# A mixed prompt and decode step: top-k masks made with ScalarE's sign pass and queued later, values in two products per key tile

## Chip, core and metric

The kernel runs on one core of a Trainium2 chip. The metric is the device time of one execution in microseconds (us). Times named "span" are the length of the profiled execution from its first to its last instruction.

## What is computed

One layer for 1024 prompt frames and 8 x 16 sampled frames that continue running streams (128 rows together, so nine tiles of 128 rows; tile 8 is the sampled one). Half of the mixing width is a gated recurrence, the other half sparse attention; both go through one output matrix, and a SwiGLU network follows. The part that the change touches is the attention. For each query row an index score is computed against all keys, and only the best 256 keys (132 for the sampled rows) take part; ties are broken by position:

```
idx_score = einsum('bths,bth->bts', relu(sc), wi)
idx_score = where(adm, idx_score, -inf)          # a chunk sees itself and what is before it
vals, sel = top_k(idx_score, topk)
s = einsum('bthgd,btkhd->bthgk', qg, ks) * HEAD_DIM ** -0.5
p = softmax(where(valid, s, -inf))
o = einsum('bthgk,btkhd->bthgd', p, vs)          # 8 query heads, 2 key/value heads of 64
...
x = x + concat([y_a, y_b]) @ w_out
x = x + (silu(gu[:, :D_FF]) * gu[:, D_FF:]) @ w_ffn_out
```

Results are wanted at float32 precision. The kernel's matmuls work on numbers split into a high and a low part, three products (low x high, high x low, high x high) for one.

## The kernel before

Work is written as generators, one per tile and stage. A planner (`run`) keeps its own clocks for the engines, steps several of them in turn and so fixes the order in which instructions are issued; a scheduler of the compiler then places them per engine. Each engine works through its own queue in that order, and an instruction that waits holds up all behind it. The stages are: norms and keys/values per tile; index scores; the recurrence and the query projections; the first half of the output projection (`out_tile_a`, the recurrence's half of w_out); attention (`attn` for eight prompt tiles times two key/value groups, `sample_attn` for eight streams); the second half of the output projection (`out_tile`); the feed-forward network. Threshold search and masks (`topk`) run beside them as side work, in two groups: tiles 2 to 5, counted on ScalarE ("act"), and tiles 6 to 8, counted on VectorE. Tiles 0 and 1 take part whole.

`topk_mask` turns the scores `s` of a tile into 0 for selected keys and -2^100 for others. With the threshold v it makes eq = (s == v) on VectorE (into the scratch `jk1` or `junk`), a running count of eq by a scan (into PSUM for tiles 2 to 5, into `key` for 6 to 8), the pass s > v with its count (VectorE, float32, in place), the number c of ties still to take (`tk_cnt`), and the selection of the first c ties; GpSimd then adds eq to s and scales:

```
nc.vector.tensor_scalar(eq, s, v, None, op0=ALU.is_equal)
nc.vector.tensor_tensor_scan(rk, e, e, a, op0=ALU.add, op1=ALU.max)
nc.vector.tensor_scalar(s, s, v, None, op0=ALU.is_gt, op1=ALU.add, accum_out=c)
nc.vector.scalar_tensor_tensor(e, rk, c, e, op0=ALU.is_le, op1=ALU.mult)
self.pool_tt(s, s, eq, ALU.add)
```

At the same time `out_tile_a` multiplies `yF` with `wa` (float32, 128x512) into two PSUM banks per tile and VectorE adds them to `acc`; `k_rope` rotates and scales the keys `kn` (VectorE and GpSimd), TensorE transposes them, ScalarE and VectorE split them into `k1` and `k2`; `q_norm` scales the queries `qn` on GpSimd. All PSUM tiles come in turn from one ring of eight banks, those of the scans too. `sample_prep` copies the mask of tile 8 (`junk<-s`) and a pattern (`key<-ident`) once all masks are there.

In `attn`, for each query tile i and group kv of four heads: scores in PSUM (`k`, `qeo`), mask and maximum on VectorE, exponentials on ScalarE, scaling on GpSimd (`m`), then for each key tile kt four transpositions, a split into high and low parts (`rest`, `smr`: ScalarE copies, VectorE subtracts), and `mm3` with the values `vhl` into one bank `po`, three matmuls of 512 columns. The stationary operand holds both groups' values, 128 columns, of which one group's 64 are used: ScalarE copies half of `po` into `yF`. Tiles 0 to 5 come first, tiles 6 and 7 among the streams.

Of the kernel before, what the change touches and what calls it, by code (L numbers as in the profile page):

```python
# [14 lines left out]
AF = mybir.ActivationFunctionType  # L15
# [6 lines left out]
NT = 9  # L22
NP = 8
# [58 lines left out]
class Kernel:  # L82
# [183 lines left out]
    def build(self, upto=99):  # L266
# [44 lines left out]
        self.jk = [self.junk.bitcast(BF16), tka_p.tile([128, widest[1]], BF16, name="jk1")]  # L311
        self.scored, self.masked, self.tk_done = set(), {0, 1}, set()
        self.qst, self.qst_t = {}, {}
        self.n_lru, self.spare = 0, None
        self.m_turn, self.m_next, self.n_sa, self.in_att, self.k_done = 0, 0, 0, False, False
        self.n_idx, self.n_sidx, self.sidx, self.sq_done = 0, 0, None, False
        topks = [self.topk(g, p) for g, p in zip(groups, self.TK_PACE)]
# [235 lines left out]
    def norm_kv(self, i, tp, g, wk):  # L553
# [25 lines left out]
        for a in range(2):  # L579
            nc.scalar.activation(sq[:, a * 64:a * 64 + 64], kv[:, a * 64:a * 64 + 64], AF.Square, scale=0.125,  # L580
                                 accum_out=self.kss[:, i, a:a + 1])
        self.hi(self.vhl[:, i, 0, :], kv[:, 128:256], "pool")
        self.lo(self.vhl[:, i, 1, :], kv[:, 128:256], self.vhl[:, i, 0, :])
        vo = O["v_p"][0, i * 128:(i + 1) * 128] if i < NP else O["v_s"].rearrange("b t k d -> (b t) k d")
        nc.sync.dma_start(vo.rearrange("t k d -> t (k d)"), kv[:, 128:256])
        nc.gpsimd.tensor_scalar(self.wi[:, i, :], kv[:, 320:328], 8.0 ** -0.5 * 64.0 ** -0.5, 0.0,
# [203 lines left out]
    def topk(self, g, pace):  # L790
# [41 lines left out]
                yield pace  # L832
        self.topk_threshold(g)
        yield pace
        for j in range(g["n"]):
            self.topk_mask(g, j)
            self.masked.add(g["tiles"][j])
            yield pace
        self.tk_done.add(g["id"])
# [45 lines left out]
    def topk_threshold(self, g):  # L885
        nc = self.nc
        v, c, t, T = g["v"], g["c"], g["t"], g["cand"].bitcast(F32)
        if not g["act"]:
            nc.vector.scalar_tensor_tensor(v, t, 2.0 ** -22, c, op0=ALU.mult, op1=ALU.add)
            nc.vector.scalar_tensor_tensor(v, v, 0.5, g["e"].bitcast(F32), op0=ALU.mult, op1=ALU.mult)  # L890
            return
        nc.vector.tensor_scalar(v, T, -1.0, None, op0=ALU.mult)
        for j, i in enumerate(g["tiles"]):
            w = self.s[i].shape[1]
            nc.vector.tensor_scalar(self.jk[1][:, :w], self.s[i], v[:, j:j + 1], None, op0=ALU.is_gt, op1=ALU.add,
                                    accum_out=c[:, j:j + 1])

        nc.vector.tensor_scalar(c, c, 256.0, 2.0 ** -24 * (1 + 2.0 ** -20), op0=ALU.is_ge, op1=ALU.mult)
        nc.vector.scalar_tensor_tensor(t, v, -1.0, v, op0=ALU.mult, op1=ALU.max)
        nc.vector.tensor_tensor(t, t, c, op=ALU.mult)  # L900
        nc.vector.tensor_tensor(v, v, t, op=ALU.add)

        nc.vector.scalar_tensor_tensor(t, v, -1.0, v, op0=ALU.mult, op1=ALU.max)
        nc.vector.tensor_scalar(t, t, 1.1754944e-38, None, op0=ALU.is_gt)
        nc.vector.tensor_tensor(v, v, t, op=ALU.mult)

    def topk_mask(self, g, j):

        nc = self.nc
        i = g["tiles"][j]  # L910
        s = self.s[i]
        w = s.shape[1]
        k = 132 if i == NP else 256
        v, c = g["v"][:, j:j + 1], g["c"][:, j:j + 1]
        eq = self.jk[1 if g["act"] else 0][:, :w]
        nc.vector.tensor_scalar(eq, s, v, None, op0=ALU.is_equal)
        rks, a = [], 0.0
        for o in range(0, w, 512 if g["act"] else w):
            e = eq[:, o:min(w, o + 512)] if g["act"] else eq
            rk = self.ps()[:, :e.shape[1]] if g["act"] else g["keys"][j]  # L920
            nc.vector.tensor_tensor_scan(rk, e, e, a, op0=ALU.add, op1=ALU.max)
            a = rk[:, -1:]
            rks.append((rk, e))
        nc.vector.tensor_scalar(s, s, v, None, op0=ALU.is_gt, op1=ALU.add, accum_out=c)
        nc.vector.tensor_scalar(c, c, -1.0, float(k), op0=ALU.mult, op1=ALU.add)
        for rk, e in rks:
            nc.vector.scalar_tensor_tensor(e, rk, c, e, op0=ALU.is_le, op1=ALU.mult)
        self.pool_tt(s, s, eq, ALU.add)
        nc.gpsimd.tensor_scalar(s, s, BIG, -BIG, op0=ALU.mult, op1=ALU.add)


# [395 lines left out]
    def out_tile_a(self, i):  # L1327

        nc = self.nc
        nc.sync.dma_start(self.acc[i], self.x_src(i))  # L1330
        w = []
        pos = [self.ps(), self.ps()]
        for c in range(4):
            w += yield from self.wait_w(("wa", c))
            for q in range(2):
                self.mm4(pos[q], self.yF[:, c, i * 128:(i + 1) * 128], w[c][:, q * 512:(q + 1) * 512], c == 0, c == 3)
            yield 0.0
        if i == NT - 1:
            self.wused -= 4
        for q in range(2):  # L1340
            a = self.acc[i][:, q * 512:(q + 1) * 512]
            nc.vector.tensor_tensor(a, pos[q], a, op=ALU.add)
            yield 0.4 if q else 0.0

    def out_tile(self, i, tp):
# [26 lines left out]
    def attn(self, i, kv, tp):  # L1372
# [57 lines left out]

        def product(kt):
            x, pT = pTs.pop(kt)
            self.mm3(po, self.vhl[:, kt, 0, :], self.vhl[:, kt, 1, :], pT[:, 0], pT[:, 1], kt == 0, kt == i)
            self.pT_free.append(x)

        for kt in range(i + 1):
# [13 lines left out]
                yield 0.0  # L1450
        yield from self.until(ready[i])
        product(i)
        a = slice(64 * kv, 64 * kv + 64)
        nc.scalar.activation(self.yF[a, :, i * 128:(i + 1) * 128], po[a].rearrange("p (j t) -> p j t", j=4), AF.Copy)

    def sample_prep(self):
        nc = self.nc
# [279 lines left out]
```

## Time and profile before

| | |
|---|---|
| median of 3 runs | 1557.31 us (1556.19 to 1558.42) |
| profiled execution | 1558.3 us, span 1556.1 us |
| mean granted TensorE clock | 0.977 of 2.4 GHz |
| busy: TensorE, VectorE, ScalarE, GpSimd | 95%, 56%, 39%, 18% |

The profiled execution is one run with its trace. Busy shares are means over stages with different limits: from about 672 us on, TensorE works on without a break and the other engines have little to do; before that VectorE and ScalarE are often the fuller ones. A busy TensorE is not one at its peak: matmuls are pipelined, and one that stands alone is counted with its whole latency. A matmul in plain float32 shows as two records. A row of the trace that ends in brackets tells how long its engine was idle before it and whose work released it.

### The profile page before, as it was taken

Reading aid. Unit: us, or ns where it says so; the run is one execution under the profiler, and the core shown is the slowest. Engines: PE = TensorE matmul, PEld = TensorE weight load, DVE = VectorE, ACT = ScalarE, POOL = GpSimd, SP = SyncE. Lnnn points to the kernel's source line nnn. Section 1 sums busy time; section 2 is a strip of 40 time slices with the busy share of each in tenths; the row PEclk is TensorE's granted clock in tenths of the full one; section 3 lists DMA queues with packets and bytes.
Section 4 is the critical chain, followed back from the end, with each engine's and each line's share of the span. In section 5 each row is a group of like instructions: output and inputs, shape, how many; then the busy total and the mean of one; then the engine's idle time right before and its main releaser. Section 6 shows DMA issues by size and latency. Waiting matters only on the chain.

```text
span 1556.1 us, 20869 instructions
## 1 busy us (share of the span) xinstructions
PE 1477.2 (95%) x7786; PEld 1313.2 (84%) x7786; DVE 876.0 (56%) x1909; ACT 613.5 (39%) x1467; POOL 274.0 (18%) x425
## 2 busy tenths in 40 slices
PE   6889899889869999999999999999999999999998
PEld 6777688778525788889999998989898989898987
DVE  7556899889986988677233333342424242414143
ACT  6447988987203977655202020212021212111100
POOL 4214233334882444300000000000000000000000
PEclk9999899999979999999999999999999999999999
DMA  7201111001400002122102020202020111111003
GB/s 240 57 16 35 42 37 30 14 21 62 163 19 16 1 15 69 28 68 73 64 0 82 0 82 1 82 2 81 16 67 27 55 40 43 49 33 55 28 1 122
DMA packets 95093, 75.24 MB, mean 48 GB/s; under 512 B 13380, under 2 KB 85828, under 8 KB 94992
## 3 DMA queue, kind: packets, MB, share of 16 engines
q1 hardware_dynamic: 94992, 73.91, 15.7%
q8 instruction: 61, 1.00, 0.3%
q14 instruction: 40, 0.33, 0.1%
HBM read 67.62 MB, written 6.27 MB: 47 GB/s over the span
## 4 chain that ended last, share of the span: by engine, by line
PE 74%; DVE 12%; ACT 7%; issue 4%; POOL 1%; DMA 1%; SPq 0%; ACTq 0%; DVEq 0%; POOLq 0%
PE ps L207 67%; DVE junk L66 4%; PE ps L212 4%; PE ps L217 3%; ACT jk L66 3%; DVE tk_cand L66 2%; ACT m L66 1%; ACT L66 1%; DVE s L66 1%; DVE tr L66 1%; ACT tr L66 1%; DVE qn L66 1%; ACT relu L66 1%; POOL qn L66 0%; DMA x<-in_x_prompt_dram 0%
## 5 line engine op out<-in xcount | busy, mean ns | idle before, releaser
L207 PE MATMUL ps<-hf,w 128*128 128x384 f32 x2556 | 460.6, 338 | 0.0
L207 PEld LDWEIGHTS ps<-hf,w 128*128 128x128 f32 x2556 | 451.5, 187 | 0.8
L207 PE MATMUL ps<-w,a 128*128 128x512 f32 x999 | 239.1, 390 | 0.0
L66 DVE TENSOR_TENSOR acc<-ps,acc 128x512 f32<-128x512 f32 x234 | 160.9, 690 | 120.4 <-PE ps L207 119.1
L207 PEld LDWEIGHTS ps<-w,a 128*128 128x128 f32 x999 | 187.4, 188 | 40.1
L66 DVE TENSOR_TENSOR sg<-ps,sg 128x384 f32<-128x384 f32 x66 | 36.8, 557 | 280.2 <-PE ps L207 279.6
L66 ACT ACTIVATE w<-raw 128x512 fp32r<-128x512 f32 x124 | 75.2, 628 | 300.2 <-PE ps L207 220.6
L66 DVE TENSOR_TENSOR w<-raw,w 128x512 fp32r<-128x512 f32 x116 | 76.8, 687 | 85.1 <-ACT w L66 84.9
L66 ACT ACTIVATE a<-sg 128x384 fp32r<-128x384 f32 x66 | 34.5, 523 | 221.2 <-DVE sg L66 221.2
L207 PE MATMUL ps<-hf,rest 128*128 128x384 f32 x612 | 114.5, 334 | 0.0
L66 ACT ACTIVATE jk<-s,tk_cand 128x384 bf16<-128x384 f32 (+3 forms) x128 | 99.4, 776 | 31.9 <-DVE tk_cand L66 29.3
L207 PE MATMUL ps<-h,w 128*128 128x384 f32 x576 | 107.3, 344 | 0.0
L207 PEld LDWEIGHTS ps<-hf,rest 128*128 128x128 f32 x612 | 106.9, 188 | 0.2
L207 PEld LDWEIGHTS ps<-h,w 128*128 128x128 f32 x576 | 101.0, 188 | 3.9 <-ACT relu L66 0.2
L207 PE MATMUL ps<-w,h 128*128 128x256 f32 (+1 forms) x600 | 95.5, 314 | 0.0
L207 PEld LDWEIGHTS ps<-w,h 128*128 128x128 f32 x600 | 82.8, 188 | 6.6
L66 ACT ACTIVATE sg<-ps 128x384 f32<-128x384 f32 x66 | 32.0, 485 | 121.9 <-PE ps L207 121.9
L212 PE MATMUL ps<-wa,yF 128*128 128x512 f32 x144 | 67.7, 626 | 3.1 <-DVE acc L66 2.2
L212 PEld LDWEIGHTS ps<-wa,yF 128*128 128x128 f32 x144 | 28.2, 202 | 38.5 <-issue 32.8
L66 POOL TENSOR_SCALAR m<-m,mx 128x128 f32<-128x128 f32 (+7 forms) x64 | 47.4, 748 | 64.7 <-DVE mx L66 57.3
L207 PE MATMUL ps<-smr,vhl 128*128 128x512 f32 x162 | 54.0, 419 | 1.3 <-ACT smr L66 1.1
L66 DVE TENSOR_TENSOR a<-sg,a 128x384 fp32r<-128x384 f32 x66 | 36.8, 557 | 32.6 <-ACT a L66 32.6
(261 smaller groups left out, 2163.7 us busy)
## 6 DMA issues: line engine op xcount, KB each, us to landing
raw<-in_w_ffn_in_dram SPq DMA_DIRECT2D x44, 512.0 KB, 4.7
raw<-in_w_ffn_out_dram SPq DMA_DIRECT2D x22, 512.0 KB, 3.6
raw<-in_w_in_dram SPq DMA_DIRECT2D x16, 512.0 KB, 5.0
out_dram<-acc SPq DMA_DIRECT2D x9, 512.0 KB, 2.6
x<-in_x_prompt_dram SPq DMA_DIRECT2D x8, 512.0 KB
acc<-in_x_prompt_dram SPq DMA_DIRECT2D x8, 512.0 KB
tab<-in_rope_dram SPq DMA_DIRECT2D x43, 64.0 KB, 1.7
wa<-in_w_out_dram SPq DMA_DIRECT2D x4, 512.0 KB
```

Source lines behind the costliest of these rows:

```text
L66: return f(*args, **kw)
L207: self.nc.tensor.matmul(out, lhsT, rhs, start=start, stop=stop)
L212: self.nc.tensor.matmul(out, lhsT, rhs, start=start, stop=stop)
L217: self.nc.tensor.transpose(out, in_, self.ident[0:n, 0:n])
```

## The change

Three things. First, a mask's equality and greater-than passes on VectorE are replaced: ScalarE computes sign(s - v) with its sum n (`topk_threshold` now leaves -v in `t` for it), VectorE compares the signs with 0, and the ties to take follow from n and the number of ties a. For tiles 2 to 5 the signs stand in s itself; for tiles 6 to 8 they stand as bf16 in the second half of the scratch `junk`, beside eq in its first half. Second, masks of tiles 6 to 8 are issued only after the last sum of `out_tile_a` (`wa_last`), in the order of every engine. Third, the values of the prompt tiles are stored as [high of a group | low of that group], 64 columns each, so that one matmul with the high part of p and one with its low part give all four products; the two halves of `po` then have to be added: ScalarE copies one half, VectorE adds the other.

```diff
@@ norm_kv
-        self.hi(self.vhl[:, i, 0, :], kv[:, 128:256], "pool")
-        self.lo(self.vhl[:, i, 1, :], kv[:, 128:256], self.vhl[:, i, 0, :])
+        v, vs = self.vhl[:, i], kv[:, 128:256]
+        if i < NP:
+            v = v.rearrange("p a (x d) -> p x a d", x=2)
+            vs = vs.rearrange("p (a d) -> p a d", a=2)
+        self.hi(v[:, 0], vs, "pool")
+        self.lo(v[:, 1], vs, v[:, 0])
@@ topk
         self.topk_threshold(g)
         yield pace
+        if not g["act"]:
+            while self.wa_last is None:
+                yield 0.5
         for j in range(g["n"]):
-            self.topk_mask(g, j)
+            with ExitStack() as st:
+                if not g["act"]:
+                    st.enter_context(self.tc.issue_after(self.wa_last))
+                self.topk_mask(g, j)
@@ topk_threshold (both groups)
+            nc.vector.tensor_scalar(t, v, -1.0, None, op0=ALU.mult)
@@ topk_mask
-        v, c = g["v"][:, j:j + 1], g["c"][:, j:j + 1]
-        eq = self.jk[1 if g["act"] else 0][:, :w]
-        nc.vector.tensor_scalar(eq, s, v, None, op0=ALU.is_equal)
+        c, eq, n = g["c"][:, j:j + 1], self.jk[1 if g["act"] else 0][:, :w], g["cnt"][:, j:j + 1]
+        sg = s if g["act"] else self.jk[0][:, 1024:1024 + w]
+        nc.scalar.activation(sg, s, AF.Sign, bias=g["t"][:, j:j + 1], accum_out=n)
+        nc.vector.tensor_scalar(eq, sg, 0.0, None, op0=ALU.is_equal)
         ...
-        nc.vector.tensor_scalar(s, s, v, None, op0=ALU.is_gt, op1=ALU.add, accum_out=c)
-        nc.vector.tensor_scalar(c, c, -1.0, float(k), op0=ALU.mult, op1=ALU.add)
+        nc.vector.tensor_tensor(c, n, a, op=ALU.subtract)
+        nc.vector.tensor_scalar(c, c, -0.5, k - 0.5 * w, op0=ALU.mult, op1=ALU.add)
         for rk, e in rks:
             nc.vector.scalar_tensor_tensor(e, rk, c, e, op0=ALU.is_le, op1=ALU.mult)
-        self.pool_tt(s, s, eq, ALU.add)
+        self.pool_tt(s, sg, eq, ALU.add)
@@ out_tile_a
-            nc.vector.tensor_tensor(a, pos[q], a, op=ALU.add)
+            x = nc.vector.tensor_tensor(a, pos[q], a, op=ALU.add)
+            if q and i == NT - 1:
+                self.wa_last = x.ins
@@ attn, product
-            self.mm3(po, self.vhl[:, kt, 0, :], self.vhl[:, kt, 1, :], pT[:, 0], pT[:, 1], kt == 0, kt == i)
+            for q in range(2):
+                self.mm(po, self.vhl[:, kt, kv], pT[:, q], kt == 0 and q == 0, kt == i and q == 1)
@@ attn, end
-        a = slice(64 * kv, 64 * kv + 64)
-        nc.scalar.activation(self.yF[a, :, i * 128:(i + 1) * 128], po[a].rearrange("p (j t) -> p j t", j=4), AF.Copy)
+        a, b = (slice(64 * x, 64 * x + 64) for x in (kv, 1 - kv))
+        y = self.yF[a, :, i * 128:(i + 1) * 128]
+        nc.scalar.activation(y, po[b].rearrange("p (j t) -> p j t", j=4), AF.Copy)
+        nc.vector.tensor_tensor(y, po[a].rearrange("p (j t) -> p j t", j=4), y, op=ALU.add)
```

Up to the end of the recurrence the order of instructions stays as it was. In VectorE's queue the first sums of the output projection stood like this before (s4 and s7: scores of tiles 4 and 7; a scan shows as SCALAR_TENSOR_TENSOR with one input):

```order
L66 SCALAR_TENSOR_TENSOR junk_911<-key_1983,tk1_cnt_905,junk_911 128x1024
L66 TENSOR_TENSOR tail_91<-tail_91 128x72
L66 TENSOR_TENSOR qn_1945<-qn_1945,tab_4134 128x256
L66 SCALAR_TENSOR_TENSOR ps_4370<-jk1_912 128x512
L66 TENSOR_SCALAR s4_890,tk0_cnt_896<-s4_890,tk0_cnt_896 128x640
L66 TENSOR_TENSOR kn_88<-kn_88,tab_4437 128x128
L66 TENSOR_TENSOR acc_4027<-ps_4360,acc_4027 128x512
L66 CAST key_1983<-ident_84 128x1024
L66 TENSOR_SCALAR tail_91<-tail_91 128x72
L66 TENSOR_TENSOR qn_1945<-qn_1945,rp_4233 128x256
L66 TENSOR_TENSOR acc_4027<-ps_4361,acc_4027 128x512
```

The same place in VectorE's queue of the changed kernel:

```order
L66 TENSOR_SCALAR jk1_912<-s5_891 128x768
L66 TENSOR_TENSOR qss_1944<-tail_91 128x72
L66 SCALAR_TENSOR_TENSOR ps_4397<-jk1_912 128x512
L66 SCALAR_TENSOR_TENSOR ps_4399<-jk1_912,ps_4397 128x256
L66 TENSOR_TENSOR acc_4007<-ps_4343,acc_4007 128x512
L66 TENSOR_TENSOR tk0_cnt_896<-tk0_cnt_896,ps_4399 128x1
L66 TENSOR_TENSOR acc_4007<-ps_4344,acc_4007 128x512
L66 TENSOR_TENSOR qn_1945<-qn_1945,tab_4169 128x256
L66 TENSOR_SCALAR tk0_cnt_896<-tk0_cnt_896 128x1
L66 TENSOR_TENSOR qn_1945<-qn_1945,rp_4257 128x256
L66 SCALAR_TENSOR_TENSOR jk1_912<-ps_4397,tk0_cnt_896,jk1_912 128x512
```

Tile 7's passes and the pattern's copy have left this place, and tile 5's have come ahead of the first sum. At the start of attention VectorE's queue went from the last sum straight to the queries' split and the first scores before:

```order
L66 TENSOR_TENSOR acc_4337<-ps_4654,acc_4337 128x512
L66 TENSOR_TENSOR ksT_4343<-ps_4685,ksT_4343 128x128
L66 TENSOR_TENSOR rest_4026<-ps_4698,rest_4026 64x4x8x16
L66 TENSOR_TENSOR qeo_4715<-ps_4710,qeo_4715 64x512 x2
L66 TENSOR_TENSOR qeo_4725<-ps_4720,qeo_4725 64x512 x2
L66 ISA m_4730,mx_4731<-ps_4732,kn_88 128x128
```

VectorE's queue at the same place now (junk and key are the scratch and the count of tile 6):

```order
L66 TENSOR_TENSOR acc_4320<-ps_4639,acc_4320 128x512
L66 TENSOR_SCALAR junk_911<-junk_911 128x896
L66 TENSOR_TENSOR ksT_4326<-ps_4670,ksT_4326 128x128
L66 SCALAR_TENSOR_TENSOR key_1983<-junk_911 128x896
L66 TENSOR_TENSOR qeo_4687<-ps_4682,qeo_4687 64x512 x2
L66 TENSOR_TENSOR tk1_cnt_905<-tk1_cnt_905,key_1983 128x1
L66 TENSOR_TENSOR qeo_4697<-ps_4692,qeo_4697 64x512 x2
L66 ISA m_4710,mx_4711<-ps_4712,kn_88 128x128
```

Tile 6's equality, scan and count now stand among the first splits and scores; those of tiles 7 and 8 follow between the scores of tiles 0 to 3. GpSimd's queue there, before, goes from filling the fixed mask of tiles 0 and 1 to the softmax scalings:

```order
L66 MEMSET kn_88 128x128
L66 MEMSET kn_88 128x256
L66 MEMSET kn_88 64x64
L66 TENSOR_SCALAR m_4730<-m_4730,mx_4731 128x128
L66 TENSOR_SCALAR m_4730<-m_4730,mx_4739 128x128
L66 TENSOR_SCALAR m_4747<-m_4747,mx_4748 128x128
```

And GpSimd's queue now:

```order
L66 MEMSET kn_88 128x256
L66 MEMSET kn_88 64x64
L66 TENSOR_TENSOR s6_892<-junk_911 128x896
L66 TENSOR_SCALAR m_4710<-m_4710,mx_4711 128x128
L66 TENSOR_SCALAR m_4710<-m_4710,mx_4727 128x128
L66 TENSOR_SCALAR m_4735<-m_4735,mx_4736 128x128
```

The mask sum of tile 6 has come ahead of the first scaling; those of tiles 7 and 8 stand between later scalings.

## Rows read from the trace of the kernel before

**Rows 1.** Busy time per engine in four stretches; columns as the second row says.
```profile
core 0: us, PE busy (x) PEld busy (x) DVE busy (x) ACT busy (x) POOL busy (x), PEclk, DMA share, GB/s
...
396.70:494.90 98.20, 78.73 (x244) 39.77 (x243) 78.52 (x157) 15.93 (x85) 63.19 (x87) 0.88 0.16 54
494.90:550.00 55.10, 49.54 (x291) 42.46 (x290) 49.50 (x175) 51.19 (x127) 22.24 (x39) 0.94 0.02 6
550.00:640.50 90.50, 88.47 (x577) 77.73 (x575) 74.61 (x212) 69.46 (x163) 42.86 (x51) 1.00 0.15 42
640.50:671.90 31.40, 28.33 (x175) 24.32 (x174) 17.68 (x38) 17.28 (x44) 4.65 (x5) 0.95 0.26 57
```

**Rows 2.** TensorE's timeline, output projection: start, duration, operation, count [idle before, releaser].
```profile
406.35 13.89 PE L212 MATMUL ps<-wa,yF 128*128 128x512 f32 x32
431.47 0.45 PE L217 MATMUL ps<-ident,kn 128*128 128x128 f32 x1 [11.23 <-DVE acc L66]
434.07 2.08 PE L212 MATMUL ps<-wa,yF 128*128 128x512 f32 x2 [2.16 <-DVE acc L66]
...
453.68 0.44 PE L217 MATMUL ps<-ident,kn 128*128 128x128 f32 x1 [5.11 <-DVE jk L66]
453.91 8.82 PE L212 MATMUL ps<-wa,yF 128*128 128x512 f32 x16
...
462.68 7.03 PE L212 MATMUL ps<-wa,yF 128*128 128x512 f32 x16
...
494.03 0.27 PE L217 MATMUL ps<-ident,kn 128*128 128x128 f32 x1
```

**Rows 3.** VectorE's groups between 396.7 and 456 us: busy, mean, idle before.
```profile
L66 DVE TENSOR_TENSOR_SCAN key<-junk 128x896 int16<-128x896 bf16 (+2 forms) x3 | 6.5, 2171 | 0.0
L66 DVE TENSOR_SCALAR_CACHE_REDUCE s<-s,tk_cnt 128x384 f32<-128x384 f32 (+6 forms) x7 | 6.2, 891 | 0.0
...
L66 DVE SCALAR_TENSOR_TENSOR junk<-key,tk_cnt,junk 128x896 bf16<-128x896 int16 (+2 forms) x3 | 4.0, 1337 | 0.0
...
L66 DVE TENSOR_SCALAR jk<-s,tk_cnt 128x384 bf16<-128x384 f32 (+3 forms) x4 | 3.1, 768 | 2.3 <-POOL s L66 2.3
...
L66 DVE TENSOR_SCALAR junk<-s,tk_cnt 128x896 bf16<-128x896 f32 (+2 forms) x3 | 1.9, 638 | 0.0
L66 DVE CAST key<-ident 128x1024 bf16<-128x1024 f32 x1 | 1.5, 1462 | 0.0
```

**Rows 4.** VectorE's timeline: one small operation twice, an accumulation.
```profile
388.35 0.43 DVE L66 TENSOR_SCALAR tk_cand<-tk_cnt 128x3 f32<-128x3 f32 x1
...
399.80 2.00 DVE L66 TENSOR_SCALAR tk_cand<-tk_cnt 128x3 f32<-128x3 f32 x1
...
430.64 0.68 DVE L66 TENSOR_TENSOR acc<-ps,acc 128x512 f32<-128x512 f32 x1
```

**Rows 5.** GpSimd's group of the mask sums of tiles 6 to 8.
```profile
L66 POOL TENSOR_TENSOR s<-s,junk 128x896 f32<-128x896 f32 (+2 forms) x3 | 6.9, 2297 | 0.1
```

**Rows 6.** GpSimd's timeline: a fill, two key tiles in turn, the first softmax scaling.
```profile
399.96 1.81 POOL L66 MEMSET rest<- 128x2048 f32 x1
...
468.53 0.40 POOL L66 TENSOR_TENSOR kn<-kn,kss 128x128 f32<-128x128 f32 x1 [0.80 <-DVE kn L66]
...
471.77 0.40 POOL L66 TENSOR_TENSOR kn<-kn,kss 128x128 f32<-128x128 f32 x1 [0.80 <-DVE kn L66]
...
501.65 3.34 POOL L66 TENSOR_SCALAR m<-m,mx 128x128 f32<-128x128 f32 x9 [6.78 <-DVE mx L66]
```

**Rows 7.** The page's group of ScalarE's counting passes for tiles 2 to 5.
```profile
L66 ACT ACTIVATE jk<-s,tk_cand 128x384 bf16<-128x384 f32 (+3 forms) x128 | 99.4, 776 | 31.9 <-DVE tk_cand L66 29.3
```

**Rows 8.** VectorE's group in attention nearest to the added sum.
```profile
L66 DVE TENSOR_TENSOR qeo<-ps,qeo 64x512 fp32r<-64x512 f32 x16 | 11.0, 689 | 2.8 <-ACT qeo L66 2.5
```

**Rows 9.** TensorE's timeline in attention: three value products, and what starts behind them.
```profile
523.79 0.86 PE L207 MATMUL ps<-smr,vhl 128*128 128x512 f32 x3
524.49 0.63 PE L207 MATMUL ps<-k,qeo 128*128 128x512 f32 x2
```

More of the change, by code (lines that the diff above doesn't have):

```diff
@@ L313, in build @@
         self.qst, self.qst_t = {}, {}
-        self.n_lru, self.spare = 0, None
+        self.n_lru, self.spare, self.wa_last = 0, None, None
         self.m_turn, self.m_next, self.n_sa, self.in_att, self.k_done = 0, 0, 0, False, False
@@ L905, in topk_threshold @@
         nc.vector.tensor_tensor(v, v, t, op=ALU.mult)
+        nc.vector.tensor_scalar(t, v, -1.0, None, op0=ALU.mult)
     def topk_mask(self, g, j):
```

## The prediction

> **What bounds the kernel now.** I read busy time by stretch first, then TensorE's timeline in the stretch that stands out, then VectorE's groups there, then the attention. The reader is to see three kinds of stretch. Before 396.7 us and after 671.9 us the change moves nothing but the layout of the values; from 671.9 us TensorE works without a break, so what is won or lost before it arrives at the end unchanged. Between them lie the first half of the output projection (396.7 to 494.9 us) and the attention (494.9 to 671.9 us).
>
> In the projection VectorE is busy 78.5 of 98.2 us and TensorE only 78.7, at a mean granted clock of 0.88; in attention up to 640.5 us TensorE is busy nearly throughout, with VectorE and ScalarE at about nine tenths in its first 55 us [rows 1]. TensorE's timeline says what the projection waits for: after two output tiles (32 records, two per fp32 matmul) it stops for 11.2 us, then 2.2, then 5.1 us, and each time VectorE releases it, by a sum into acc or by a mask pass that frees a PSUM bank [rows 2]. VectorE does not idle in that time: the masks of tiles 2 to 8 are queued ahead of the sums [rows 3], so that the first sum starts at 430.64 us [rows 4], ten us after TensorE had finished its input at 420.24.
>
> **Masks moved out of the projection.** Up to the first sum VectorE loses, for tiles 6 and 7, two scans (2.17 us each), two equality passes (0.64) and two selections (1.34): 8.3 us; and for tiles 2, 3, 4, 6 and 7 the greater-than pass with its count, 5 x 0.89 = 4.5 us [rows 3]. It gains, by the order, tile 5's equality (0.77) and scan, which used to stand behind the sums (at the scan's rate for a mean of 816 columns, 2.0 us for 768), and three one-column subtractions (under the 0.43 us of a 128x3 operation [rows 4]; taken at 0.15). That is 12.8 - 3.3 = 9.5 us: the first sum starts near 421, its bank is free near 422, and TensorE's first wait falls from 11.2 to about 1.6 us. Between the first two sums stood a 1.5 us copy, which now follows the masks; that wait falls below 1 us. The wait of 5.1 us was for a bank that tile 5's mask held; it is now given back before the next tile's sums. I leave 2 us there, because the key tiles come from GpSimd, whose queue lies close behind. GpSimd loses 6.9 us of mask sums [rows 5], and its chain per key tile, once alone, takes 471.77 - 468.53 = 3.24 us [rows 6], nine of them 29 us, under the projection's 63.
>
> So 18.5 us of waits become 4.6, a gain of 13.9. The first records behind the long waits ran at the lower of the two clocks, 1.2 GHz: 2.08 us for 2 records where 0.88 is the rate at 2.4 GHz, and 8.82 for 16 instead of 7.03 [rows 2]; with short waits these 3.0 us go too. Sum: **-17 us**. The ceiling is TensorE without any wait, 9 x 7.03 = 63.3 us for 144 records against 494.03 - 406.35 = 87.7: -24.4. The other end is -8, if only the first wait shrinks, and GpSimd's key and query work is then late.
>
> ScalarE gets seven sign passes at about 0.78 us, the price of its counting passes [rows 7]. Those of tiles 2 to 6 come while it is busy 15.9 of 98.2 us [rows 1]: nothing, unless the square passes behind them free banks too late for the last query tiles, at most their 4 us.
>
> **Masks moved into the attention.** The order puts all VectorE work of tiles 6 to 8 behind the last sum, between the score passes of tiles 0 to 3: scans 6.5, selections 4.0, equality 1.9 (that is the fp32 price; on bf16 signs it can only be less, down to nothing), six one-column operations 0.9 (as above), and two mask copies at up to 1.5 each [rows 3]: 16.3 us. The new sum into yF is closest to the 64x512 subtraction at 0.69 us [rows 8], sixteen times: 11.0 us, half in tiles 0 to 3. So VectorE gets 21.8 us more where it was busy 49.5 of 55.1 us [rows 1]: between +16.2 (all its idle time filled) and +21.8. I take +17, near the filled end, since no other engine gets much more to do there. In this also hides the start: GpSimd's first softmax scaling, at 501.65 us before [rows 6], now waits in its queue behind the 2.3 us mask sum of tile 6 [rows 5], and that for VectorE's three passes; ScalarE's sign pass of tile 7 waits for the same sum, with exponentials behind it, since all three tiles share one scratch.
>
> **Two products instead of three.** 36 tiles of keys times two groups: 72 matmuls of 512 columns less. Three take 524.49 - 523.79 = 0.70 us, 0.233 each [rows 9]: 16.8 us of TensorE, 4.7 in tiles 0 to 3, 10.2 in 550 to 640.5 us (44 products), 1.9 in the last eight. In 550 to 640.5 TensorE goes from 88.5 to 78 busy us and VectorE from 74.6 to 80.1, so VectorE becomes the longest queue [rows 1]. The stretch can fall from 90.5 to 80 at best; at the share VectorE reached in the first 55 us (0.90) it would be 89. I take 83.5: -7. The tail after 640.5 us, with little VectorE work, gives the 1.9: -2. The floor is no gain at all, if VectorE's and ScalarE's hand-overs set the pace. Early, the 4.7 us hide behind VectorE and count nothing.
>
> The values' split write in the first 75 us has as many elements as before; nothing, at worst nine times the 0.40 us of a 128x128 GpSimd pass [rows 6].
>
> **Sum.** -17 + 17 - 7 - 2 = -9 us. The profiled execution took 1558.3 us (span 1556.1 and 2.2 around it), 1.0 over the median of 1557.3; 1558.3 - 9 - 1 gives **1548 us**.
>
> **Rivals.** *Attention is TensorE's alone.* Then VectorE's added work fills gaps, and all 16.8 us of products count, less about 5 us for the late first scaling: -17 - 12 = -29, 1528 us. For it: 88.5 of 90.5 us busy [rows 1]. Against: a busy TensorE here includes the latency of single matmuls, and VectorE has only 5.6 us free in the first 55.
>
> *The masks choke the softmax (slower).* Place: VectorE, GpSimd and ScalarE from the last projection sum to tile 3. If VectorE keeps its old shares, the first part takes (49.5 + 21.8) / 0.90 = 79, +24, and the next (74.6 + 5.5) / 0.82 = 97, +7: +31 - 17 = +14, 1571 us. It decides as soon as attention grows by more than the projection gains. For it: VectorE and GpSimd can hold each other up. An operation of three columns took 2.00 us at 399.80, beside GpSimd's fill of 1.81 us from 399.96, and 0.43 otherwise [rows 4, 6]. The masks' scans would come among GpSimd's scalings. Against: other work can fill in at every one of these places.
>
> The Trainium skill, "SBUF — State Buffer", section "Who interferes with whom", has a rule for it: VectorE's two-port modes, or two SBUF inputs against a reading GpSimd, share one port pair, and whoever comes second is blocked for the whole instruction. The 2.00 us agree in size; by that rule the moved passes would pay more in attention than their rows say, which is this rival.
>
> *GpSimd is the projection's next bound.* If the key tiles, queued behind query scalings and mask sums, come late for the third transposition, the gain is the -8 above and attention still pays its +8: 1557 us.
>
> **How the numbers follow.** Forecast 0.55 (its own range 1541 to 1555); TensorE's attention 0.15; choking 0.13; GpSimd 0.17. The range for 8 in 10 runs from 1536, part of the way to 1528, to 1562, part of the way to 1571. A measurement here tells about 0.2% (3.1 us) from no change: faster means under 1554.2, which holds for most of the forecast (0.51), the first rival (0.15) and a third of the last (0.06): 0.72. Same gets 0.12, mostly from the last rival; slower the choking and the rest: 0.16.
>
> **What would show it.** First sum near 421 us and its transposition's wait under 3 us; last projection matmul near 477 (470 to 486) instead of 494. Then value products 144 instead of 216 at 0.23 us, VectorE over 95% busy in the first 60 us of attention, and the attention from last projection matmul to the last yF piece 8 us longer than before. I am wrong if attention is shorter (the first rival), if it grows by 17 or more (the second), or if TensorE's waits before the third key tile stay above 5 us (the third).

## The result and the profile after

The changed kernel takes 1567.76 us (median of 4 runs, 1564.87 to 1570.28) where the kernel before takes 1557.82 on the same chip: 1.0065 of it, interval 1.0044 to 1.0085. That is slower, where 1548 was forecast. Its profiled execution took 1570.28 us, span 1568.2.

I divide both traces at four events that both have: TensorE's first `wa` matmul, the last transposition of keys ahead of the attention, the last product of values, and the network's first matmul (`hf,w`). The three stages between them are called projection, attention and tail. Busy time per stage, kernel before, then the changed kernel (columns as in [rows 1]):

```profile
406.35:494.03 87.68, 68.21 (x155) 29.30 (x154) 68.19 (x129) 10.23 (x42) 57.18 (x79) 0.86 0.11 33
494.03:669.59 175.56, 164.90 (x1035) 143.49 (x1033) 141.18 (x421) 136.57 (x331) 70.21 (x96) 0.97 0.13 32
669.59:721.07 51.48, 51.32 (x253) 42.58 (x252) 42.14 (x91) 28.49 (x53) 0.00 (x0) 1.00 0.17 50
```

```profile
408.32:474.31 65.99, 63.18 (x154) 27.67 (x153) 44.77 (x100) 10.23 (x42) 39.19 (x68) 1.00 0.11 34
474.31:672.00 197.69, 164.71 (x953) 138.71 (x952) 160.51 (x451) 139.27 (x333) 81.78 (x104) 0.90 0.10 26
672.00:732.77 60.77, 55.49 (x263) 45.29 (x262) 44.20 (x93) 29.18 (x55) 0.00 (x0) 0.97 0.18 51
```

The projection is 21.7 us shorter, the attention 22.1 us longer, and the tail, in which nothing was changed, 9.3 us longer; the first stage starts 2.0 us later. That is +11.7 of the span's 12.1 us. In the attention TensorE is busy as long as before, 164.7 us, with 82 matmuls fewer (72 products, and ten that now come later): its mean clock there is 0.90 instead of 0.97, and a mean score product takes 394 ns where it took 370.

TensorE's projection after, against [rows 2]:

```profile
408.32 13.89 PE L212 MATMUL ps<-wa,yF 128*128 128x512 f32 x32
422.06 0.27 PE L217 MATMUL ps<-ident,kn 128*128 128x128 f32 x1
...
424.41 2.84 PE L212 MATMUL ps<-wa,yF 128*128 128x512 f32 x6 [1.22 <-DVE tk_cnt L66]
...
439.25 0.33 PE L217 MATMUL ps<-ident,kn 128*128 128x128 f32 x1 [1.58 <-POOL kn L66]
...
474.31 0.27 PE L217 MATMUL ps<-ident,kn 128*128 128x128 f32 x1
```

The three waits of 11.2, 2.2 and 5.1 us have become none, 1.2 and 1.6. VectorE's first sum, at 430.64 in [rows 4], and the moved work of [rows 3] now read so:

```profile
423.69 0.67 DVE L66 TENSOR_TENSOR acc<-ps,acc 128x512 f32<-128x512 f32 x1
...
475.12 0.38 DVE L66 TENSOR_SCALAR junk<-junk 128x896 bf16<-128x896 bf16 x1
...
475.62 2.01 DVE L66 TENSOR_TENSOR_SCAN key<-junk 128x896 int16<-128x896 bf16 x1
...
482.05 1.15 DVE L66 SCALAR_TENSOR_TENSOR junk<-key,tk_cnt,junk 128x896 bf16<-128x896 int16 x1
...
491.94 0.65 DVE L66 TENSOR_TENSOR tk_cnt<-tk_cnt,key 128x1 f32<-128x1 f32 x1
...
496.79 0.67 DVE L66 CAST key<-ident 128x1024 bf16<-128x1024 f32 x1
```

The masks of tiles 6 to 8 start with the attention. What that does to TensorE's start there:

```profile
478.40 4.57 PE L207 MATMUL ps<-k,qeo 128*128 128x128 f32 x18 [2.94 <-DVE qeo L66]
485.56 0.48 PE L217 MATMUL ps<-ident,m 128*128 128x128 f32 x1 [2.59 <-POOL m L66]
```

The first transposed probabilities come 11.3 us after the last transposition of keys (before: 502.08 less 494.03, 8.1). The tail after shows four rows that the kernel before has not:

```profile
673.90 8.52 PE L207 MATMUL ps<-w,rest 128*128 128x512 f32 x36 [1.50 <-ACT w L66]
684.02 3.00 PE L207 MATMUL ps<-w,rest 128*128 128x512 f32 x12 [1.61 <-DVE rest L66]
689.20 1.33 PE L217 MATMUL ps<-ident,xs 128*128 128x128 f32 x8 [2.17 <-DVE xs L66]
690.19 9.94 PE L207 MATMUL ps<-w,rest 128*128 128x512 f32 x36
```

### The profile page after: what moved, and what is told of

The parts are those of the page before. It is cut to its first block, busy times and chain, and to the rows that moved or that the text cites. A ratio compares the mean times of both kernels' runs of the same rounds, so it can differ in the third digit from the quotient of the medians.

```text
span 1568.2 us, 20771 instructions
## 1 busy us (share of the span) xinstructions
PE 1478.9 (94%) x7714; PEld 1312.5 (84%) x7714; DVE 875.2 (56%) x1920; ACT 621.1 (40%) x1481; POOL 269.2 (17%) x425
## 4 chain that ended last, share of the span: by engine, by line
PE 69%; DVE 14%; ACT 7%; issue 5%; POOL 2%; DMA 2%; SPq 0%; POOLq 0%; ACTq 0%; DVEq 0%
PE ps L207 63%; DVE junk L66 4%; PE ps L212 3%; PE ps L217 3%; ACT jk L66 3%; DVE tk_cand L66 2%; DVE m L66 1%; ACT L66 1%; DVE smr L66 1%; DVE tr L66 1%; POOL rp L66 1%; DVE ti L66 1%; ACT tr L66 1%; ACT relu L66 1%; ACT m L66 1%
## 5 line engine op out<-in xcount | busy, mean ns | idle before, releaser
L212 PE MATMUL ps<-wa,yF 128*128 128x512 f32 x144 | 63.2, 593 | 1.2 <-DVE tk_cnt L66 1.2
L217 PE MATMUL ps<-ident,m 128*128 128x128 f32 x288 | 50.4, 301 | 8.9 <-POOL m L66 7.1
L207 PE MATMUL ps<-k,qeo 128*128 128x384 f32 (+5 forms) x192 | 54.5, 394 | 4.4 <-DVE qeo L66 3.7
L66 ACT ACTIVATE m<-m,mx 128x128 f32<-128x128 f32 (+7 forms) x64 | 49.4, 772 | 19.2 <-DVE mx L66 18.9
```

Of the source, the lines that this page charges most:

```text
L66: return f(*args, **kw)
L207: self.nc.tensor.matmul(out, lhsT, rhs, start=start, stop=stop)
L212: self.nc.tensor.matmul(out, lhsT, rhs, start=start, stop=stop)
L217: self.nc.tensor.transpose(out, in_, self.ident[0:n, 0:n])
```

## The experiments

Every run was timed beside the kernel before; a difference is the change of the median against it. "Attention" and "tail" are the stages above in the run's own trace, one execution each.

| run | vs before, us | ratio (interval) | attention | VectorE busy in it | tail |
|---|---|---|---|---|---|
| before | | | 175.6 | 141.2 | 51.5 |
| changed kernel | +9.9 | 1.0065 (1.0044, 1.0085) | 197.7 | 160.5 | 60.8 |
| e1 values alone | +14.5 | 1.009 (1.0075, 1.0105) | 184.3 | 148.8 | 60.5 |
| e2 masks alone | -10.6 | 0.9925 (0.9908, 0.9942) | 186.9 | 152.8 | 51.5 |
| e3 sign pass alone | +1.6 | 1.001 (1.0, 1.0019) | 176.4 | 141.6 | 51.5 |
| e4 later place alone | -6.4 | 0.9955 (0.9941, 0.997) | 190.5 | 155.6 | 51.7 |
| e5 values, order of three | +9.0 | 1.0052 (1.0036, 1.0069) | 184.2 | 148.9 | 52.3 |
| e6 values, no sum | +9.0 | 1.0049 (1.0031, 1.0067) | 171.9 | 138.8 | 60.5 |
| e7 values, third product | +12.9 | 1.0075 (1.0055, 1.0094) | 188.8 | 151.2 | 51.5 |
| e8 before, order of two | +11.3 | 1.0066 (1.0049, 1.0083) | 176.9 | 140.6 | 58.9 |
| e9 sum on own data | +15.4 | 1.0101 (1.0085, 1.0118) | 182.1 | 149.6 | 60.6 |
| e10 sum of one column | +12.8 | 1.008 (1.0065, 1.0095) | 178.4 | 141.6 | 59.1 |
| e11 changed, order of three | -1.3 | 1.0 (0.9983, 1.0018) | 194.3 | 160.3 | 52.3 |
| e12 sum on GpSimd | -4.2 | 0.9971 (0.9958, 0.9985) | 190.3 | 153.2 | 52.3 |
| e13 masks, order of two | -2.8 | 0.9983 (0.9974, 0.9992) | 187.7 | 151.7 | 59.0 |
| e14 no sum, charged | +8.9 | 1.0057 (1.0042, 1.0072) | 175.0 | 139.2 | 60.6 |
| e15 before, order shifted | +5.0 | 1.0033 (1.0022, 1.0044) | 173.2 | 140.1 | 59.0 |
| e16 masks later still | -6.4 | 0.9959 (0.9945, 0.9973) | 188.2 | 152.1 | 51.5 |

One trace tells small differences only with care. In ten kernels of the table (before, e1, e5 to e10, e14, e15) all four engines' queues are the same up to the last transposition of keys, and still the first `wa` matmul starts anywhere from 403.23 to 408.91 us and the projection takes 85.3 to 88.3 us; so the 2.0 us by which the changed kernel's first stage starts later can't be put down to the change. Where the queues stay the same nearly to the end of the attention, it repeats closely: e15's sixteen copies of prompt tiles into `yF` come within 0.1 us of those of the kernel before, counted from the start of the stage, up to the last one at 177.2 us. Set against the kernel before, attention and tail together give the difference of the medians within 0.5 us in five of these kernels; e1's trace gives 3.2 us more, e6's 3.6, e8's 2.6 and e10's 2.3 us less.

**The parts alone.** e1 has only the edits to `norm_kv` and `attn`, e2 only those to the masks, e3 of these only `topk_threshold` and `topk_mask`, e4 only `issue_after` with the old mask passes; each is the diff of the change with the other places left as before.

> Of the change only the values: two products of 512 columns per tile of keys, and the sum of both halves into yF on VectorE; the masks stay as before. The new kernel's attention, from the last projection matmul to the last product of values, took 22 us more than before (197.7 for 175.6), while the projection gained 19.7; which part of the change that comes from is what this run tells. Theory A (the moved masks fill VectorE at the start of attention, the values' part is as forecast): this kernel is 5 to 10 us faster than before, about 1549, the attention 7 to 9 us shorter, first acc sum still near 430. Theory B (the sum into yF costs more than a third of the products saves: TensorE was not what attention waited for, and a bank of PSUM is held through two engines): 4 to 10 us slower, about 1564, with the attention longer by as much. In between (1554 to 1560): neither alone.

> Of the change only the masks: sign pass on ScalarE, the masks of tiles 6 to 8 queued behind the last projection sum; the values keep three products and no sum into yF. Projection near 474 at its last transposition in any case. Theory A (masks choke the softmax): the attention takes back all of the 20 us or more, 1557 to 1566. Theory B (the values' part did the damage): attention grows by 8 to 12 us only, 1545 to 1550. Theory C (any later place of tile 8's mask delays the decode samples, which end the attention): as A, but the samples' last product comes later than before relative to the last prefill tile, and TensorE waits for GpSimd at the samples' transpositions.

> Of the change only the sign pass on ScalarE in place of VectorE's counting pass; the masks stay where they were, values as before. VectorE loses 7 passes of 0.89 us ahead of or between the projection's sums and gains seven one-column operations: the first acc sum 3 to 5 us earlier than 430.6, attention unchanged: 1552 to 1555 by theory A and B alike. If it is no faster or slower (1557 or more), ScalarE's sign pass is a hop on the way of a mask (VectorE waits for it), which then holds in the new kernel too.

> Of the change only the later place: the old mask passes of tiles 6 to 8, all of them on VectorE, queued behind the last projection sum; values as before. Projection: three scans, selections and passes less in front of the sums: last transposition at 476 to 480. Attention gets 15 us of VectorE work. Theory A: slower than the kernel with the sign pass by about the 2.7 us of three counting passes, 1558 to 1568. Theory B: attention hides half of it, 1546 to 1553.

e1 is as slow as theory B said and more; e2 is faster than the kernel before, its attention 11.4 us longer. So the masks gain and the values lose. The sign pass alone does nothing that can be told (both theories had 3 to 5 us): its projection is 2.8 us shorter, and begins 4.3 us later; its queues differ from those of the kernel before from 336 us on, where the changed kernel's still agree, so the late start can belong to another order of the recurrence as well. The later place alone makes six tenths of e2's gain. e2 by stage:

```profile
406.13:472.42 66.29, 63.18 (x154) 27.67 (x153) 45.05 (x100) 10.26 (x42) 39.53 (x68) 1.00 0.12 35
472.42:659.35 186.93, 171.21 (x1035) 147.30 (x1033) 152.76 (x438) 138.77 (x335) 83.33 (x104) 0.93 0.11 31
659.35:710.84 51.49, 51.33 (x254) 42.57 (x253) 41.98 (x90) 28.50 (x53) 0.00 (x0) 1.00 0.17 49
```

**Order or work.** `mm` adds each matmul's time to the planner's clock. e5, e8 and e11 change that charge alone, each in another kernel (e1, the one before, the changed one); e6 leaves the sum out, e7 puts the third product back:

```diff
 # e5 and e11, after the two products; e8, after mm3 of the kernel before
+            self.pe += 512 / 2400.0          # e5, e11: charge three, issue two
+            self.pe -= 512 / 2400.0          # e8: charge two, issue three
 # e6
-        nc.vector.tensor_tensor(y, po[a].rearrange("p (j t) -> p j t", j=4), y, op=ALU.add)
 # e7
-            for q in range(2):
-                self.mm(po, self.vhl[:, kt, kv], pT[:, q], kt == 0 and q == 0, kt == i and q == 1)
+            for n, q in enumerate((0, 1, 1)):
+                self.mm(po, self.vhl[:, kt, kv], pT[:, q], kt == 0 and n == 0, kt == i and n == 2)
```

> The values' part alone, as in the run that was 14.5 us slower than before, but the planner that writes out the order charges each tile of keys the time of three products while two are issued. Theory O (order: the planner's clock is TensorE's work; with a product less it puts less TensorE work between a softmax and the transpositions that wait for it, and TensorE then stands still): 8 to 15 us faster than the values' part under its own order, 1557 to 1564, with fewer waits for GpSimd's samples. Theory V (the sum into yF, 11 us of VectorE and a PSUM bank held through two engines, is the price): within 3 us of 1572.

> The values' part alone, without the sum into yF: the products of one part of the values are computed and left in PSUM, so the output holds the other part only. VectorE has 16 operations of 0.69 us less and the bank comes free at the copy. Theory V: back at or under the kernel before, 1553 to 1560. Theory O: still 8 us or more slower than before, 1566 to 1574.

> The values' part alone with a third product per tile of keys issued again (the low part of the probabilities a second time, so that part counts twice in the output): TensorE's work as before, the sum into yF stays. Theory V: no better than two products, 1570 to 1580. Theory O: the planner's order is close to that of before, and only the sum is added: 1557 to 1564. Theory K (with less work TensorE falls to 1.2 GHz in its waits, and the third product keeps it at 2.4): as O, but with a granted clock near 0.98 in 550 to 672 us where the two-product kernel shows 0.90 to 0.95.

> The kernel before, all its work unchanged (three products, no sum into yF), but the planner charges two products per tile of keys, so that the order of all engines is written out as if there were two. Theory O: slower than before by 5 to 15 us, 1563 to 1572. Theories V and K: within 3 us of 1558.

Neither O nor V held alone. The stages part them: attention follows the sum (184.3 with it, 171.9 without, 188.8 with sum and third product), the tail follows the charge (51.5 to 52.3 with three, 58.9 to 60.6 with two), whether two or three products are issued. Theory K is out: with the third product back the granted clock in the attention is 0.95 where e1 has 0.92, and the attention is longer all the same. e8 does the work of before, and loses 11.3 us by the order alone; in its trace the tail has 7.4 of that and the attention 1.3. e6 leaves the removed product by itself:

```profile
491.53:663.40 171.87, 150.20 (x953) 130.09 (x952) 138.84 (x419) 136.67 (x329) 70.19 (x96) 0.95 0.11 30
```

TensorE is busy 14.7 us less than before, and the attention is 3.7 us shorter: the rest has become waits. In the whole times, with the same charge on both sides, the removed product gives 2.3 us (e6 against e8) and 3.9 (e5 against e7). The sum can be read from e7, which has TensorE's work and charge of before and the sum, with its charge on VectorE, on top: it takes 12.9 us longer than the kernel before.

```profile
492.55:681.38 188.83, 172.49 (x1034) 147.27 (x1033) 151.24 (x436) 136.76 (x331) 70.52 (x96) 0.95 0.12 30
```

**The price of the sum.** e9 lets VectorE add data that nobody writes there, e10 lets it wait for ScalarE's copy and the bank (the hop) but add one column of 128, e14 leaves the sum out and keeps its charge:

```diff
 # e9
+        scr = tp.tile([128, 512], F32, tag="scr", name="scr", bufs=1)
+        own = self.acc[NT - 1][a, 0:512]
+        nc.vector.tensor_tensor(scr[a], own, own, op=ALU.add)
 # e10
+        nc.vector.tensor_tensor(y[:, :, 0:1], po[a].rearrange("p (j t) -> p j t", j=4)[:, :, 0:1], y[:, :, 0:1], op=ALU.add)
+        self.busy["vector"] += 508 * 0.00104
 # e14
+        self.busy["vector"] = max(self.busy["vector"], self.now()) + 0.07 + 512 * 0.00104
```

> The values' part alone, but VectorE's sum takes its operands from a tile in SBUF that nobody writes in this stage (the output holds one half of the values' products): VectorE's 16 operations of 0.69 us stay in its queue, while no PSUM bank and no copy of ScalarE is waited for. From the last transposition of keys to the last product of values the attention took 175.6 us before, 184.3 with the values' part, 171.9 with it and no sum. Theory T (the sum costs VectorE's time): 182 to 186, whole time 1569 to 1574. Theory H (it costs the hop: VectorE waits for ScalarE's copy, the bank of PSUM is held until the sum): 171 to 175, whole time 1561 to 1566. The tail behind the attention stays at 60 us by both, since the planner charges two products.

> The other half of the pair: VectorE's sum reads the bank and waits for ScalarE's copy, but adds one column in 128 only (four of 512; the rest of the output holds one half of the products), and the planner is charged the whole operation. Theory T: attention 172 to 176 us, whole time 1561 to 1566. Theory H: 182 to 186, 1569 to 1574.

> The values' part alone without the sum into yF, but with its time still charged to VectorE in the planner (the output holds one half of the values' products). Without the charge the attention took 171.9 us, with charge and a sum of one column 178.4, with the whole sum 184.3. If execution is the price: 171 to 174. If the order that the charge brings about is: 177 to 180. The whole time follows: 1564 to 1567, or 1569 to 1572.

Against e14 (175.0) the attention grows by 3.4 us with the hop and one column (e10), and by 9.3 with the whole sum (e1). The sums stand at much the same places in e10 and e1 (first at 15.9 us into the stage in both, last at 182.2 and 187.9), and their mean length is 161 and 686 ns, so the 5.9 us between them would be VectorE's time. But the whole times rank the steps the other way: 8.9, 12.8 and 14.5 us over the kernel before, each with an interval of more than 2 us to either side. That the sum costs is shown; how its price divides between VectorE's time and the hop is not. e10 came between its forecasts in attention, and where theory H had it in the whole time.

e9, with no hop, costs 7.1 us of attention and 6.5 of whole time against e14. But its sixteen additions did not run where the sums do. All of them started in the first 33 us of the attention, among the first softmax work:

```profile
L66 DVE TENSOR_TENSOR scr<-acc x16: 673/690/977, 492.8 to 525.7; 64x512 f32<-64x512 f32 x16
```

So it shows that 11.4 us of VectorE's time alone have a price at the start of the stage, and not what the sum's time costs at its own places. e14 came between its two forecasts, a little nearer to execution. Its attention is 3.1 us longer than e6's, which would be the order that the charge brings about, but the whole times do not show that (8.9 and 9.0 us over the kernel before).

**The tail, and how much a shift of the order does.** e11 is the changed kernel with the charge of three, e13 is e2 with the charge of two, e15 is the kernel before with `self.pe += 0.02` per tile of keys.

> The changed kernel, except that the planner charges three products per tile of keys for the two that are issued. Theory O2 (the charge of two moves one tile's half of the output projection behind the end of attention: from the last product of values to the network's first matmul 51.5 us before, 60.8 in the changed kernel; with the values' part alone the charge of three brought it from 60.5 to 52.3): 51 to 53 here, the attention within 2 us of 197.7, whole time 1557 to 1562. If the tail stays near 60, it hangs on more than the charge.

> The masks' part alone (1547.2 us: attention 186.9, tail from the last product of values to the network's first matmul 51.5) with three products done, but two charged by the planner. Theory O2 (the charge of two alone moves one tile's half projection behind the attention): tail 58 to 61, whole time 1554 to 1560. If the tail stays at 51 to 53 and the time within 3 us of 1547, the 9 us need the missing products themselves.

> The kernel before, all work unchanged, the planner charging 0.02 us more per tile of keys (72 times, 1.4 us in all): a control for how much the order alone moves the time. If the order of before is one of many as good: within 3 us of 1557.5. If it is a lucky one: 1561 to 1568, and then a part of every difference here is the price of another order and not of the work.

The tails of e11 and e13 came as theory O2 had them (e11's attention is 3.4 us under the changed kernel's, and its time a little under the forecast). So of the changed kernel's time the charge of two is 11.2 us, with the same work done: +9.9 against -1.3. e11's attention and tail:

```profile
473.41:667.74 194.33, 164.42 (x965) 137.47 (x964) 160.26 (x453) 139.78 (x335) 81.92 (x104) 0.90 0.11 29
667.74:720.01 52.27, 50.66 (x250) 42.00 (x249) 42.47 (x92) 28.16 (x53) 0.00 (x0) 1.00 0.17 49
```

e15 is the control: 1.4 us of charge in all, and the tail is the long one, so the order of before is a lucky one there. Its attention is 2.4 us shorter only because work has moved from it into the tail. TensorE at the end of the attention there, then in the kernel before:

```profile
666.58 0.63 PE L207 MATMUL ps<-smr,vhl 128*128 128x512 f32 x2
667.85 8.52 PE L207 MATMUL ps<-w,rest 128*128 128x512 f32 x36 [0.64 <-ACT w L66]
676.52 3.00 PE L207 MATMUL ps<-w,rest 128*128 128x512 f32 x12 [0.16 <-DVE rest L66]
681.98 1.89 PE L217 MATMUL ps<-ident,xs 128*128 128x128 f32 x8 [2.46 <-issue]
683.52 9.40 PE L207 MATMUL ps<-w,rest 128*128 128x512 f32 x36
```

```profile
669.59 0.62 PE L207 MATMUL ps<-smr,vhl 128*128 128x512 f32 x2
670.05 6.12 PE L207 MATMUL ps<-w,rest 128*128 128x512 f32 x26
676.33 8.48 PE L207 MATMUL ps<-w,rest 128*128 128x512 f32 x36 [0.16 <-DVE rest L66]
684.65 1.91 PE L217 MATMUL ps<-ident,xs 128*128 128x128 f32 x16
```

In the kernel before, 62 records of the second projection stand ahead of the first transposition of normed rows `xs`, which then finds two tiles ready (16 matmuls); in the other order 48 stand there, one tile is transposed (8), and TensorE waits for it and for the weights `w`, then runs on partly at the lower clock (9.40 us for 36 records at a granted 0.90; 8.49 at 1.00 before). Ten records that before lay in gaps of the attention come after it, too: 204 instead of 194 in the changed kernel and in e15, some 2.4 us at 8.48 for 36.

**Two versions that might have been better.** e12 is e11 with the sum on GpSimd, e16 is e2 with `wa_last` set by ScalarE's copy of tile 1's second group:

```diff
 # e12
+        sm = tp.tile([128, 512], F32, tag="sm", name="sm", bufs=2)
+        nc.scalar.activation(sm[a], po[a], AF.Copy)
+        nc.gpsimd.tensor_tensor(y, sm[a].rearrange("p (j t) -> p j t", j=4), y, op=ALU.add)
 # e16, in attn
+        if (i, kv) == (1, 1):
+            self.wa_last = x.ins
```

> A version that may beat both: masks as in the changed kernel, two products, charge of three, and the sum into yF made by GpSimd from two ScalarE copies of 64 x 512, so that VectorE gets nothing and the bank is free after ScalarE. The kernel with the masks alone and three products stands at 1547.2 (attention 186.9, tail 51.5). Theory T (VectorE's time is the price of the sum, and ScalarE's 16 further copies of 0.4 us and GpSimd's 16 sums find room): attention 181 to 186, 1540 to 1546. If ScalarE sets the pace together with VectorE, or GpSimd's sums stand in front of the softmax scalings: attention 188 to 194, 1548 to 1555.

> The masks' part alone, three products, but the masks of tiles 6 to 8 are queued only behind ScalarE's copy of tile 1's second group into yF, some 35 us into the attention, instead of behind the last projection sum. If their price lies at the start (first transposition of probabilities 11 us after the last transposition of keys with them in front, 8 before): the first tiles run as before, the attention takes 178 to 183 instead of 186.9, whole time 1539 to 1544. If VectorE's time is the price wherever the masks stand: 185 to 189, 1545 to 1550. If the decode streams, which need the mask of tile 8, come too late: 190 or more.

Neither beats e2. e12 takes the sum from VectorE, whose time falls by 7.1 us against e11, and the attention by 4.0 only, with ScalarE 7.0 us and GpSimd 20.2 us longer. In e16 the start is free again (first transposed probabilities 7.1 us after the last keys, from its rows at 478.25 and 471.17, instead of 11.3), and the attention is about as long as in e2. Its sixth copy into `yF` comes 37.1 us into the stage, as before the change (36.8; e2 48.0), its tenth at 78.1, as in e2 (before 67.5): the masks cost their ten microseconds wherever they stand. e16's profiled execution is the fastest of its five, so its stages do not hold the 4 us by which its median is behind e2's. The fastest kernel of all is e2, the masks' part with three products: 1547.23 us.

## Why the prediction was wrong

**"Masks moved out of the projection", -17: right, and a little small.** The projection lost 21.7 us (21.4 in e2). The first sum came at 423.69 (421 forecast), the last transposition at 474.31 (477), the waits were 0, 1.2 and 1.6 us (1.6, under 1, 2); the clock is 1.00 instead of 0.86. The values' split write costs nothing that a trace can tell: in e1 the projection begins at 405.99, before at 406.35. The third rival, GpSimd as the next bound, is out: TensorE's wait before the third key tile is 1.6 us, where more than 5 would have been its sign.

**"Masks moved into the attention", +17 with half of the sums: the masks' share was right in size.** e2 shows 11.4 us for the masks alone; of the 21.8 us of VectorE's work that I priced, 16.3 were masks, and at +17 for all that is 12.7. The trace gives them 11.6 us of VectorE's time (152.8 - 141.2); the pattern copy, for one, takes 0.67 us and not 1.46 [rows 3]. What I named as the reason, a start held up by the queues, is there (VectorE was busy 51.2 of the 55 us from 475 us on, 93%) but does not decide: e16 takes it away and gains nothing.

**"Two products instead of three", -7 - 2, and the sum beside it: this step failed.** The forecast for the values' part is -9 and the other 4.3 us of the +17, near -5; e1 measured +14.5, and e5, the same work in the order of three, +9.0. The miss of 20 us adds up about like this: with the charge of three the parts add (-10.6 in e2 and +9.0 in e5 are -1.6; both together, e11, are -1.3), and the charge of two, which the change brought with it, is the 11.2 us between e11 and the changed kernel. Against the forecast the masks did 6 us better than their share, the values' work 14 us worse, and the order, which the forecast did not have, took 11.

Three things in the step were wrong. I let the late stretch fall with TensorE's busy time (88.5 to 78) until VectorE would be full; the removed product gave 2.3 to 3.9 us of 16.8. I let half of the sums, those behind tile 3, cost nothing until VectorE would be full; but the sum costs 9.3 us of attention in the trace of e1 against that of e14 (5.6 in whole times, and 12.9 in e7), 4.7 up to the eighth copy into `yF` (tiles 0 to 3) and 4.6 after it, so not only where VectorE was nine tenths busy. And I wrote that after 671.9 us "the change moves nothing": the order of the second projection did move, by the planner's charge, and the tail grew by 9.3 us.

**The rivals.** "The masks choke the softmax" supposed that VectorE keeps its old shares, and that is what happened (0.93 in the first 55 us of attention and 0.83 in the next 90.5, where it had 0.90 and 0.82): the attention grew by 22.1 us, more than the 17 that the forecast had named as this rival's sign, 14.1 of them up to the eighth copy into `yF`. But the masks are not what made the kernel slower: alone (e2) they gain 10.6 us. That its 1571 us are near the 1567.8 is luck: its 31 us of attention were 22.1, and the tail's 9.3, which it did not know, make up for them. "Attention is TensorE's alone" is refuted by e6.

**VectorE's share.** In all eighteen kernels of the table VectorE is busy 79 to 83% of the attention (141.2 of 175.6 before, 160.5 of 197.7 after, 138.8 of 171.9 in e6), while TensorE's busy time goes from 150 to 172 us. ScalarE's busy time hardly moves beside that (135.5 to 139.9 us in all but e12), so it is not what lengthens the stage. A straight line through the eighteen pairs rises by about 1.05 us of attention for one on VectorE; single pairs go from 0.6 (e11 and e12) to 1.3 (e7 and the kernel before), and their orders differ too. I had taken the nine tenths of the first 55 us for the limit and a TensorE busy 88.5 of 90.5 us for the bound. Why the share stops at 0.8 is argued, not shown: at each hand-over (VectorE waits for ScalarE's exponentials and copies, TensorE for both) some tenths of a microsecond are lost in a fixed order.

The rule that I cited from the Trainium skill, "SBUF — State Buffer", section "Who interferes with whom", shows in one place after: the subtraction of one column at 491.94 took 0.65 us, beside a GpSimd pass from 491.97 (0.61 us); the one before of its kind took 0.16. It agrees with the rule. But the moved passes as a whole did not pay more in the attention than their rows said, as that rival had it; they paid less: the three scans took 2010 ns on average where they took 2171, the three selections 1135 where they took 1337 [rows 3].

## What to carry to other kernels

Work taken from one engine counts only where that engine's time sets the stage; look for the engine whose busy share stays the same when the stage grows or shrinks, and price every added operation on it, here at about one for one. Where a planner writes the order from estimated costs, a changed estimate moves work in stages that the edit does not touch: time the kernel before with only the estimate changed before a loss is put down to the work. And take a change of several parts apart: here one part gains 0.75% (e2), the other loses 0.5% by its work (e5), and the order that comes with it takes 0.7% (e11).

## What the runs showed that was not expected

TensorE's busy time did not fall with its work list: with 82 matmuls fewer it was busy as long as before (164.7 us), at a granted clock of 0.90 instead of 0.97. Whether the lower clock made the attention longer is not shown; e7, with the clock nearly back, is no shorter. And a shift of 1.4 us in the planner's estimates, with no work changed, moved the whole time by 5.0 us (1.0022 to 1.0044), more than the 0.2% that the forecast had called a measurement's limit.
